# A two-layer encoder on one core: norms, weight splits, residual means and the last transposes in another order

## The chip, the cores and the metric

One core of a Trainium2 chip runs the whole kernel in one launch. The metric is the device time of that launch in microseconds. One core has TensorE (PE in the rows, with its weight loads as PEld), VectorE (DVE), ScalarE (ACT), GpSimd (POOL) and SyncE (SP); the last three can issue DMA transfers, each on a queue of its own. L611 means line 611 of the kernel before, unless the text says that it is a line of the changed one.

## The reference, cut to what matters

```python
def layer_norm(x, gain, bias):
    mean = jnp.mean(x, -1, keepdims=True)
    var = jnp.mean(jnp.square(x - mean), -1, keepdims=True)
    return (x - mean) * lax.rsqrt(var + LN_EPS) * gain + bias

def swiglu_ffn(h, w_gate, w_up, w_down):
    return (jax.nn.silu(h @ w_gate) * (h @ w_up)) @ w_down

# s5_mixer: y = C state + D u; g = gelu(y); (g * sigmoid(g @ w_glu)) @ w_out
h = concat(meta, x)                      # 16 + 1024 rows of 1024 values
for i in range(2):
    mix = s5_mixer(h, ...) if i == 0 else gqa_mixer(h, ...)
    h = layer_norm(ALPHA * h + mix, gain[i, 0], bias[i, 0])
    h = layer_norm(ALPHA * h + swiglu_ffn(h, ...), gain[i, 1], bias[i, 1])
return h[:, 16:]
```

D_FF is 2816. The inputs and all weights are float32.

## The kernel before, in words

The activations live in SBUF transposed, `acc` with 8 slices `k` of 128 features by 1040 tokens. All products run over three token tiles of 348, 348 and 344 columns (`TOK`, tiles 0, 1, 2). For accuracy every operand is a pair of a high part (rounded to fp32r) and a low part (the rest), and each of the 8 k-steps of a product takes three matmuls: high by high (L694), high by low (L695), low by high (L696). A bank of PSUM (`bk`) collects a product. `Hh` and `Hl` are the two parts of the activations.

In order of time: an S5 phase (to about 292 us) that ends with the C times state matmuls (L533, added by DVE in L535); the GLU product; the S5 output product with norm `ln0` (to about 500); FFN 0 with norm `ln1` (to about 1260); the products for K, V and Q; attention; its output product with norm `ln2` (to about 2050); FFN 1 with norm `ln3`; and the transposes and stores of the output (from about 2808).

**Order.** Nothing is scheduled by a planner: each engine executes its instructions in the order in which the program issues them. Work beside the products is written as generators. `Net.group_done` is called after each half product (four k-steps) and counts every generator down by 1.75, by 0.9 in the FFN's down products and the V rows; a generator whose count is used up runs to its next `yield`, whose value is the next count. `flush` runs a generator to its end at once. A larger number in a `yield` thus places what follows it behind more matmuls on PE's queue.

**Weights** (`class Weights`). SP loads 128 x 1024 pieces (`raw`, L592); `split` makes a unit: the high part by an ACT cast (L609) and the low part by a subtraction (L611) on DVE, or on POOL for four units of the K and V weights (`on_pool`). The w_down units are centred: ACT sums a row (L606) and writes the high part (L616), DVE the low part (L617). `tick`, called at each whole product, splits the next unit when its buffer is free.

**Norm** (`layer_norm`, one generator for each token tile). Per slice, ACT squares (L721) and POOL adds into `lns` (L723, even and odd slices apart). After a `yield` PE sums over the partitions by a matrix of ones (L735 for `s`, L736 for `q2`), ACT loads the table of ln and exp (L737) and with DVE makes 1/sqrt (L706 to L710); then for each slice DVE scales (L750), ACT writes `Hh` (L751), DVE `Hl` (L745). The mean needs no pass ahead of it since the weights and residuals are centred. For the residual the mean is taken out of `acc` later (`residual`): POOL adds the eight slices to `lnz` (L764), PE sums by ones (L768), DVE subtracts (eight L771), and in `ln1` POOL issues a save of the tile to DRAM (L774). In the last norm ACT writes into `acc` in L751 and the transposes read it.

**GLU.** The y of the S5 phase goes to DRAM (`ydram`, L543) and comes back in another layout (L554) for gelu. The last pair of feature tiles comes back late, when the GLU product already runs on the first ones (Hh by ACT in L784, Hl by DVE in L788). `centre_x` subtracts the mean from x beside it (POOL sums `sx` in L1361, PE sums by ones in L1368).

**Tail.** For each token tile the norm is flushed, then each block of 128 tokens takes two banks of four transposes (L1534); DVE copies one to `ot` (L1538), ACT the other (L1536), and SP stores the block (L1539). There are three `ot` buffers.

Of the kernel before, what the change touches and what calls it, by code (L numbers as in the profile page):

```python
# [9 lines left out]
FP32 = mybir.dt.float32  # L10
# [102 lines left out]
def s5_phase(nc, tc, P, a, ident, acc, xres, ydram, late):  # L113
# [413 lines left out]
    for ft in range(KT):  # L527
        for g0 in range(8 * ft, 8 * ft + 8, 2):
            b = bank()
            for j in range(2):  # L530
                g = g0 + j
                for c2 in range(2):
                    PE.matmul(b[:, j * NK:(j + 1) * NK], E(c2, g).rearrange("p s c -> p (s c)"), XS[:, :, c2, g],  # L533
                              start=(c2 == 0), stop=(c2 == 1))
            V.tensor_tensor(out=U[:, g0:g0 + 2, :], in0=U[:, g0:g0 + 2, :],  # L535
                            in1=b[:, :2 * NK].rearrange("p (g k) -> p g k", g=2), op=ALU.add)
        for _ in range({1: 2, 7: 1}.get(ft, 0)):
            split()
        if ft % 2:
            dst = ydram[(ft - 1) * 128:(ft + 1) * 128].rearrange("(g c) t k -> t c g k", c=CH)  # L540
            for t in range(T):
                eng = nc.gpsimd if t % 4 == 3 else nc.sync
                eng.dma_start(out=dst[t], in_=U[16 * t:16 * t + 16, 8 * ft - 8:8 * ft + 8, :])  # L543
            if ft < LATE_FT:
                for f in (ft - 1, ft):
                    ys[f] = load_y(nc.scalar, y_p, ydram, f)
                for f in (ft - 1, ft):
                    gelu(nc, acc, ys[f], f)
# [17 lines left out]
class Weights:  # L566


    def __init__(self, nc, n_units, n_raw):
        self.nc, self.nu, self.nr = nc, n_units, n_raw  # L570
        self.src = []
        self.centre = {}
        self.on_pool = set()
        self.raw = []
        self.unit = []
        self.free = []
        self.base = 0
        self.limit = 10 ** 6
# [7 lines left out]
    def dma(self):  # L586
        while len(self.raw) < min(len(self.src), len(self.unit) + self.nr):
# [7 lines left out]
            self.raw.append(r)  # L595

    def split(self):
        n = len(self.unit)
        self.dma()
# [8 lines left out]
        if c is False:  # L608
            A.copy(out=u[:, 0], in_=r)  # L609
            E = self.nc.gpsimd if n in self.on_pool else V  # L610
            E.tensor_tensor(out=u[:, 1], in0=r, in1=u[:, 0].bitcast(FP32), op=ALU.subtract)  # L611
        else:
# [6 lines left out]
        self.unit.append(u)  # L619
        self.dma()  # L620

    def tick(self):
        n = len(self.unit)
        if n < min(len(self.src), self.limit) and (n < self.nu or self.free[n - self.nu]):
            self.split()

    def get(self, n):
        while len(self.unit) <= n:
            assert len(self.unit) < self.nu or self.free[len(self.unit) - self.nu], (len(self.unit), n)
            self.split()  # L630
        return self.unit[n]

# [20 lines left out]
class Net:  # L653
    def __init__(self, nc, tc, P, a):
        self.nc, self.tc, self.P, self.a = nc, tc, P, a
        self.bg = []
        self.ln_s = {}


    def group_done(self, work=HALF, tick=True):  # L660

        if tick:
            self.w.tick()
# [11 lines left out]
    def start(self, gen, key):  # L675
        it = [gen, 0, key]
        self.bg.append(it)
        self.bg_step(it)
        return it

    def flush(self, key):
# [43 lines left out]
    def layer_norm(self, tok, ln, last=False, save=None):  # L725
# [6 lines left out]
        s, q2 = self.ln_s[tok, 0], self.ln_s[tok, 1]  # L732
        yield (3,3,3)[tok] if ln == 1 else 3.0
        v = self.bank()[:, :n]
        PE.matmul(v, self.ones, s, start=True, stop=False)  # L735
        PE.matmul(v, self.ones, q2, start=False, stop=True)  # L736
        A.preload_act_table_set("natural_log_exp_and_others")  # L737
        u = self.rstd(v, self.eps_ln, n, tp)

        def bias(k):  # L740
# [17 lines left out]

        def residual():

            yield (20.,20.,20.)[tok] if ln == 1 else 28.0
            sz = tp.tile([128, 348], FP32, tag="s", name="lnz", bufs=2)[:, :n]
            for k in range(1, KT):
                PO.tensor_tensor(out=sz, in0=x[0] if k == 1 else sz, in1=x[k], op=ALU.add)  # L764
                yield 0.9
            yield 4.0
            mz = self.bank()[:, :n]
            PE.matmul(mz, self.ones, sz, start=True, stop=True)  # L768
            for k in range(KT):
                b = self.bias_c[:, 8 * ln + k:8 * ln + k + 1]  # L770
                V.scalar_tensor_tensor(out=x[k], in0=x[k], scalar=b, in1=mz, op0=ALU.add, op1=ALU.subtract)  # L771
                yield 0.9
            if save is not None:
                nc.gpsimd.dma_start(out=save.rearrange("(k p) t -> p k t", p=128)[:, :, t0:t0 + n],  # L774
                                    in_=acc[:, :, t0:t0 + n])

        if not last:
            self.start(residual(), ("lnb", tok))

# [61 lines left out]
    def ffn(self, i, units, ln, last=False, save=None):  # L841
# [22 lines left out]
        def down(c, gt, t):  # L864
            ud = units[c][2]
            t0, n = TOK[t]
            if c == 0:
                self.flush(("lnb", t))
            for o in range(KT):
# [361 lines left out]
def whole(nc, tc, a, out):  # L1231
# [37 lines left out]
    uv = N.add_square(wq, 1280)  # L1269
    w.on_pool.update((uk + uv)[:4])  # L1270
    uq = [N.add_square(wq, 256 * i) for i in range(2)]
# [188 lines left out]
    def q_evac(o, t, b):  # L1460
        N.flush(("lnb", t))
        t0, n = TOK[t]
# [61 lines left out]
    for t in range(3):  # L1524
        N.flush(("ln", t))
        t0, n = TOK[t]
        c0 = max(t0, 16)
        while c0 < t0 + n:
            m = min(128, t0 + n - c0)
            ot = outp.tile([128, D], FP32, tag="ot", name="ot")  # L1530
# [58 lines left out]
```

## Time and profile before

| what | value |
|---|---|
| median of 3 runs | 2845.06 us (2843.23 to 2846.6) |
| profiled execution, own time | 2844.93 us |
| its span, first to last instruction | 2843.2 us |
| PE busy | 2649.4 us, 93% |
| DVE, ACT, POOL busy | 55%, 41%, 18% |
| mean granted clock of PE | 0.967 of full speed |

The profile gives one profiled execution. An engine is busy while it executes; its idle time ahead of an instruction is put down to what released it. A row with "[4.25 <-ACT Hh L784]" says that the engine sat idle 4.25 us before it, until ACT's write of Hh in L784 was done. PEclk is the clock that PE was granted, 1.00 at 2.4 GHz and 0.50 at 1.2 GHz.

### The profile page before, as it was taken

The page shows a single profiled execution, that of the slowest core. Times are in us where ns is not written, and L with a number is a line of the kernel's source. Part 1 is how long each engine was busy: PE and PEld are TensorE (multiplying, and loading weights), DVE is VectorE, ACT ScalarE, POOL GpSimd, SP SyncE. Part 2 cuts the span into 40 slices and gives each one's busy share as a digit, 9 for nine tenths or more (in the row PEclk, how much of TensorE's full clock was granted, in tenths as well). Part 3 has the DMA queues.
Part 4 walks back from the last instruction along what each step waited for, and adds up shares of the span by engine and source line. Part 5 has one row for each costly group of instructions (what it writes and reads, how often), then busy time and mean ns, then how long its engine had stood idle before and what let it go on. Part 6 is the DMA issues. An engine that isn't in the chain of part 4 may idle for free.

```text
span 2843.2 us, 43155 instructions
## 1 busy us (share of the span) xinstructions
PE 2649.4 (93%) x17277; PEld 2546.5 (90%) x17277; DVE 1559.1 (55%) x3025; ACT 1154.3 (41%) x2138; POOL 515.3 (18%) x533
## 2 busy tenths in 40 slices
PE   7657899999999999989999998999999999999997
PEld 6446899999999999988988887888999999999996
DVE  9994545733333333358768888885563333333334
ACT  7463534322212212245557778774522222222225
POOL 0770332300000000043034434431310000000002
PEclk9778999999999999999999999999999999999998
DMA  6113652221111111112111111102111111111101
GB/s 150 24 38 102 230 175 72 77 80 45 47 51 45 45 52 45 45 45 87 48 24 39 27 24 49 28 19 98 45 38 46 52 45 45 45 45 45 45 31 60
DMA packets 124836, 167.41 MB, mean 59 GB/s; under 512 B 13499, under 2 KB 104971, under 8 KB 124635
## 3 DMA queue, kind: packets, MB, share of 16 engines
q1 hardware_dynamic: 118203, 141.22, 17.5%
q0 software_dynamic: 5712, 21.30, 2.2%
q8 instruction: 136, 2.23, 0.3%
q10 hardware_dynamic: 720, 2.13, 0.2%
q14 instruction: 65, 0.53, 0.1%
HBM read 126.41 MB, written 21.23 MB: 52 GB/s over the span
## 4 chain that ended last, share of the span: by engine, by line
PE 78%; DVE 13%; ACT 4%; issue 3%; DMA 2%; POOL 1%; SPq 0%; ACTq 0%; DVEq 0%; POOLq 0%
PE bk L694 22%; PE bk L695 22%; PE bk L696 22%; PE pv L1106 4%; PE pt L1084 3%; DVE mx L1064 3%; DVE pl L1097 2%; PE b L533 2%; ACT ph L1092 1%; DVE TA L507 1%; DVE SB L508 1%; DVE XS L510 1%; PE bx L347 1%; PE b L124 1%; DVE TS L509 1%
## 5 line engine op out<-in xcount | busy, mean ns | idle before, releaser
L694 PE MATMUL bk<-Hh,unit 128*128 128x348 f32 (+1 forms) x2928 | 956.4, 327 | 9.4 <-ACT Hh L784 5.8
L695 PE MATMUL bk<-Hl,unit 128*128 128x348 f32 (+1 forms) x2928 | 945.3, 323 | 1.1 <-DVE Hl L788 1.0
L696 PE MATMUL bk<-Hh,unit 128*128 128x348 f32 (+1 forms) x2928 | 943.8, 322 | 0.0
L694 PEld LDWEIGHTS bk<-Hh,unit 128*128 128x128 f32 x2928 | 555.2, 190 | 14.7 <-ACT Hh L784 5.4
L695 PEld LDWEIGHTS bk<-Hl,unit 128*128 128x128 f32 x2928 | 554.9, 190 | 6.4 <-DVE Hl L788 2.0
L696 PEld LDWEIGHTS bk<-Hh,unit 128*128 128x128 f32 x2928 | 554.7, 189 | 0.0
L858 DVE TENSOR_TENSOR sg<-sg,bk 128x348 f32<-128x348 f32 x132 | 68.1, 516 | 632.3 <-PE bk L696 624.5
L723 POOL TENSOR_TENSOR lns<-lns,lnsq 128x348 f32<-128x348 f32 (+1 forms) x72 | 70.0, 983 | 1550.5 <-ACT lnsq L721 1549.4
L694 PE MATMUL bk<-gt,unit 128*128 128x348 f32 (+1 forms) x1056 | 340.5, 322 | 0.0
L696 PE MATMUL bk<-gt,unit 128*128 128x348 f32 (+1 forms) x1056 | 339.1, 321 | 0.0
L695 PE MATMUL bk<-gt,unit 128*128 128x348 f32 (+1 forms) x1056 | 338.5, 321 | 0.0
L881 DVE TENSOR_TENSOR acc<-acc,bk 128x348 f32<-128x348 f32 (+1 forms) x480 | 237.5, 513 | 112.7 <-PE bk L696 112.7
L860 ACT CAST gt<-sg 128x348 fp32r<-128x348 f32 x132 | 63.7, 482 | 487.6 <-DVE sg L858 487.6
L1084 PE MATMUL pt<-ident,P 128*116 128x128 f32 (+1 forms) x1188 | 181.3, 279 | 44.1 <-DVE pl L1097 39.4
L1097 DVE TENSOR_TENSOR pl<-pt,ph 116x512 fp32r<-116x512 f32 (+3 forms) x340 | 204.4, 619 | 15.0 <-ACT ph L1092 13.4
L1084 PEld LDWEIGHTS pt<-ident,P 128*116 128x116 f32 (+1 forms) x1188 | 132.5, 136 | 80.4 <-issue 30.6
L1072 POOL TENSOR_SCALAR P<-P,l 128x1044 f32<-128x1044 f32 x132 | 149.8, 1146 | 291.0 <-PE pv L1106 174.4
L694 PEld LDWEIGHTS bk<-gt,unit 128*128 128x128 f32 x1056 | 199.0, 188 | 0.5 <-issue 0.2
L695 PEld LDWEIGHTS bk<-gt,unit 128*128 128x128 f32 x1056 | 198.9, 188 | 0.5 <-issue 0.2
L696 PEld LDWEIGHTS bk<-gt,unit 128*128 128x128 f32 x1056 | 198.7, 188 | 0.0
L1092 ACT CAST ph<-pt 116x512 fp32r<-116x512 f32 (+3 forms) x340 | 168.6, 535 | 73.9 <-PE pt L1084 59.7
L609 ACT CAST unit<-raw 128x1024 fp32r<-128x1024 f32 x110 | 113.2, 1046 | 209.7 <-DMA raw<-in_ffn_w_up_dram 173.1
(287 smaller groups left out, 3928.1 us busy)
## 6 DMA issues: line engine op xcount, KB each, us to landing
raw<-in_ffn_w_gate_dram SPq DMA_DIRECT2D x44, 512.0 KB
raw<-in_ffn_w_up_dram SPq DMA_DIRECT2D x44, 512.0 KB
raw<-in_ffn_w_down_dram SPq DMA_DIRECT2D x44, 512.0 KB
y<-xdram SPq DMA_DIRECT2D x16, 520.0 KB
QA<-QH SPq DMA_DIRECT2D x30, 260.0 KB
raw<-in_attn_w_qkv_dram SPq DMA_DIRECT2D x14, 512.0 KB
xdram<-acc SPq DMA_DIRECT2D x32, 130.0 KB
xres<-xn POOLq DMA_DIRECT2D x8, 520.0 KB, 5.1
```

The source lines that it names most:

```text
L609: A.copy(out=u[:, 0], in_=r)
L694: mm(out, wh, xh, start=(first and i == 0), stop=False)
L695: mm(out, wh, xl, start=False, stop=False)
L696: mm(out, wl, xh, start=False, stop=(last and i == n - 1))
L723: (nc.vector if on_dve else nc.gpsimd).tensor_tensor(out=part, in0=part, in1=sq, op=ALU.add)
L881: V.tensor_tensor(out=x, in0=x, in1=b, op=ALU.add)
L1064: V.tensor_reduce(out=k.mx, in_=k.S[:, :, :348], axis=mybir.AxisListType.XY, op=ALU.max, negate=True)
L1072: PO.tensor_scalar(out=k.P, in0=k.P, scalar1=k.l, scalar2=1.0, op0=ALU.mult, op1=ALU.mult)
L1084: PE.transpose(b[:m, w * i + 128 * x:w * i + 128 * x + 128], u.P[x][:, KB_N * kt:KB_N * kt + m], self.ident)
L1092: A.copy(out=u.ph[s][:m, :w], in_=u.t[s][:m, :w])
L1097: V.tensor_tensor(out=u.pl[s][:m, :w], in0=u.t[s][:m, :w], in1=u.ph[s][:m, :w].bitcast(FP32), op=ALU.subtract)
L1106: PE.matmul(u.o[:, :u.w], VAs[u.j][:m, kt], (u.ph, u.pl)[x][s][:m, c:c + u.w], start=(kt == 0 and x == 0), stop=(kt == KBS - 1 and x == 1))
```

## The change

Six edits, all in the order of the work; no matmul is added or removed.

1. The eight stores of the last pair of y tiles (`ft` = 7) go round SP, POOL and ACT (3, 3 and 2 of them); before, SP issued six and POOL two. The two on ACT stand ahead of its first `Hh` casts.
2. `split` issues the cast at once, but the subtraction for the low part and the next load of raw weights only in `finish`, which the next `group_done`, `split` or `get` of the unit calls. The subtractions on POOL (`on_pool`) are gone: all are on DVE.
3. The first wait of a norm stays 3.0 for tiles 0 and 1, and becomes 7.0 (ln0, ln2) or 5.0 (ln1, ln3) for tile 2. On PE, L735 and L736 of tile 2 stand 16 k-steps behind the end of its product instead of 8 in ln0 and ln2, and 12 instead of 8 in ln1. Meanwhile `hold` keeps units of w_down from being split.
4. The three residual generators become one chain, started at the end of tile 2's norm, in the order of tiles 2, 0, 1, with shorter waits. On PE at the start of an FFN, L768 of tile 2 stands 40 k-steps behind tile 2's L736, that of tile 0 28 k-steps later and that of tile 1 24 further; in the K, V, Q stage L768 of tile 2 stands behind 16 k-steps of tile 1, tile 0's inside tile 2's K products and tile 1's inside the Q products.
5. `flush_res(t)` runs the chain until tile t is done, in place of a flush of that tile's own generator.
6. In the tail `begin` starts the waiting norm of tile 2 after the first block of tile 1.

```diff
-                eng = nc.gpsimd if t % 4 == 3 else nc.sync
+                eng = (nc.sync, nc.gpsimd, nc.scalar)[t % 3] if ft == KT - 1 else nc.gpsimd if t % 4 == 3 else nc.sync
...
+    def finish(self):
+        while self.later:
+            self.later.pop(0)()
+
     def split(self):
+        self.finish()
...
             A.copy(out=u[:, 0], in_=r)
-            E = self.nc.gpsimd if n in self.on_pool else V
-            E.tensor_tensor(out=u[:, 1], in0=r, in1=u[:, 0].bitcast(FP32), op=ALU.subtract)
+            self.later.append(lambda: V.tensor_tensor(out=u[:, 1], in0=r, in1=u[:, 0].bitcast(FP32), op=ALU.subtract))
...
-        self.dma()
+        self.later.append(self.dma)
...
     def tick(self):
         n = len(self.unit)
+        if self.hold and n in self.centre and self.centre[n] is None:
+            return
...
     def group_done(self, work=HALF, tick=True):
 
+        self.w.finish()
...
+    def begin(self, key):
+
+        for it in list(self.bg):
+            if it[2] == key and it[1] > 0 and it not in self.begun:
+                self.begun.append(it)
+                self.bg_step(it)
...
-        yield (3,3,3)[tok] if ln == 1 else 3.0
+        self.w.hold = tok == 2
+        yield 3.0 if tok < 2 else 5.0 if ln % 2 else 7.0
...
-            yield (20.,20.,20.)[tok] if ln == 1 else 28.0
...
-                yield 0.9
-            yield 4.0
+                yield 0.5
+            yield 3.0
...
-                yield 0.9
+                yield 0.6
...
-        if not last:
-            self.start(residual(), ("lnb", tok))
+            self.res_done.add(t)
+
+        def residuals():
+
+            yield 2.0
+            for t in (2, 0, 1):
+                yield from residual(t)
+
+        if not last and tok == 2:
+            self.res_done = set()
+            self.start(residuals(), "lnb")
+
+    def flush_res(self, t):
+
+        for it in list(self.bg):
+            while it[2] == "lnb" and it in self.bg and t not in self.res_done:
+                self.bg_step(it)
...
             if c == 0:
-                self.flush(("lnb", t))
+                self.flush_res(t)
...
-    w.on_pool.update((uk + uv)[:4])
...
     def q_evac(o, t, b):
-        N.flush(("lnb", t))
+        N.flush_res(t)
...
         while c0 < t0 + n:
+            if t == 1 and c0 > t0:
+                N.begin(("ln", 2))
```

How instructions stand on an engine, at three places. Lines of the changed kernel are its own: there L612 is L606 of before, L615 is L609, L621 is L616, L724 to L726 are L706 to L708, L739 is L721, L741 is L723, L756 is L737, L771 (on ACT) is L751, L785 is L764, L795 is L774, L892 and L895 (Silu and its cast) are L857 and L860, L1572 is L1536.

ACT at the start of an FFN (here ln0; ln2 reads the same), from the last square of tile 2 on; before:

```order
L721 ACTIVATE lnsq<-acc 128x344
L606 ACTIVATE unit,mean<-raw 128x1024
L616 ACTIVATE unit<-raw,mean 128x1024
L606 ACTIVATE unit,mean<-raw 128x1024
L616 ACTIVATE unit<-raw,mean 128x1024
L737 ACT_TABLE_LOAD
L706 ACTIVATE rs_y<-bk,eps_ln 128x344
L707 ACTIVATE rs_y<-rs_y 128x344
L708 ACTIVATE rs_u<-rs_y 128x344
L751 ACTIVATE Hh<-acc,small 128x344 x4
```

and changed:

```order
L739 ACTIVATE lnsq<-acc 128x344
L612 ACTIVATE unit,mean<-raw 128x1024
L621 ACTIVATE unit<-raw,mean 128x1024
L892 ACT_TABLE_LOAD
L892 ACTIVATE sg<-bk 128x348
L895 CAST gt<-sg 128x348
L756 ACT_TABLE_LOAD
L724 ACTIVATE rs_y<-bk,eps_ln 128x344
L725 ACTIVATE rs_y<-rs_y 128x344
L726 ACTIVATE rs_u<-rs_y 128x344
L771 ACTIVATE Hh<-acc,small 128x344 x2
L612 ACTIVATE unit,mean<-raw 128x1024
```

One pair of weight copies moved behind the first two writes of Hh, and a first Silu group of FFN tile 0 with a table load of its own stands ahead of the norm's table load.

POOL from the sums of tile 1 in ln1 to the residual adds of the K, V, Q stage; before:

```order
L723 TENSOR_TENSOR lns<-lns,lnsq 128x348 x3
L611 TENSOR_TENSOR unit<-raw,unit 128x1024
L723 TENSOR_TENSOR lns<-lns,lnsq 128x344 x3
L611 TENSOR_TENSOR unit<-raw,unit 128x1024
L723 TENSOR_TENSOR lns<-lns,lnsq 128x344 x3
L1450 DMA cos<-in_rope_cos_dram 128x1040
L1451 DMA sin<-in_rope_sin_dram 128x1040
L764 TENSOR_TENSOR lnz<-acc 128x348
L764 TENSOR_TENSOR lnz<-lnz,acc 128x348 x6
L774 DMA hres<-acc 128x8x348
```

and changed:

```order
L741 TENSOR_TENSOR lns<-lns,lnsq 128x348 x12
L741 TENSOR_TENSOR lns<-lns,lnsq 128x344 x6
L1484 DMA cos<-in_rope_cos_dram 128x1040
L1485 DMA sin<-in_rope_sin_dram 128x1040
L785 TENSOR_TENSOR lnz<-acc 128x344
L785 TENSOR_TENSOR lnz<-lnz,acc 128x344 x6
L795 DMA hres<-acc 128x8x344
L785 TENSOR_TENSOR lnz<-acc 128x348
L785 TENSOR_TENSOR lnz<-lnz,acc 128x348 x6
L795 DMA hres<-acc 128x8x348
```

The subtractions left POOL, and each save of a tile now stands ahead of the adds of the next one; before, the adds of the tiles 1 and 2 stood together ahead of their saves.

ACT in the tail, from the last writes of tile 1 on; before:

```order
L751 ACTIVATE acc<-acc,small 128x348 x2
L1536 COPY ot<-bk 128x512 x2
L1536 COPY ot<-bk 92x512
L737 ACT_TABLE_LOAD
L706 ACTIVATE rs_y<-bk,eps_ln 128x344
L707 ACTIVATE rs_y<-rs_y 128x344
L708 ACTIVATE rs_u<-rs_y 128x344
L751 ACTIVATE acc<-acc,small 128x344 x8
```

and changed:

```order
L771 ACTIVATE acc<-acc,small 128x348 x2
L1572 COPY ot<-bk 128x512
L756 ACT_TABLE_LOAD
L724 ACTIVATE rs_y<-bk,eps_ln 128x344
L725 ACTIVATE rs_y<-rs_y 128x344
L726 ACTIVATE rs_u<-rs_y 128x344
L771 ACTIVATE acc<-acc,small 128x344 x2
L1572 COPY ot<-bk 128x512
L1572 COPY ot<-bk 92x512
L771 ACTIVATE acc<-acc,small 128x344 x6
```

The copies of blocks 2 and 3 of tile 1 moved from ahead of tile 2's norm into the middle of its writes.

## Rows read from the trace of the kernel before

**Rows 1.** The page, busy time of each engine, share of the span, instructions.

```profile
PE 2649.4 (93%) x17277; PEld 2546.5 (90%) x17277; DVE 1559.1 (55%) x3025; ACT 1154.3 (41%) x2138; POOL 515.3 (18%) x533
```

**Rows 2.** Waits of PE; waited for: us in total, times, longest.

```profile
PE bk L1534 <- ACT acc L751: 11.4, 4, 7.9
PE bk L735 <- POOL lns L723: 11.3, 4, 4.7
PE bk L736 <- POOL lns L723: 6.7, 2, 3.3
PE bk L694 <- ACT Hh L784: 5.8, 3, 4.2
...
PE bk L694 <- ACT vf L1476: 3.6, 1, 3.6
```

**Rows 3.** Stretches of PE: from:to, us, busy (instructions), granted clock, DMA share, GB/s.

```profile
315.90:322.70 6.80, 4.17 (x13) 0.50 0.41 143
500.20:507.00 6.80, 5.23 (x16) 0.50 0.33 100
1258.00:1261.40 3.40, 3.40 (x10) 0.50 0.22 77
1271.60:1278.40 6.80, 6.00 (x17) 0.50 0.46 163
1295.50:1298.90 3.40, 3.16 (x11) 0.50 0.00 0
2049.90:2056.70 6.80, 5.67 (x18) 0.50 0.34 101
530.00:1225.00 695.00, 695.00 (x4387) 1.00 0.16 51
```

**Rows 4.** Timeline, GLU: start, us, engine, line, shapes, count, [idle before, releaser].

```profile
294.09 5.46 SPq L543 DMA_DIRECT2D ydram<-acc  x6
...
307.33 1.05 POOL L554 DMA_DIRECT2D y<-ydram  x2 [11.17 <-DMA ydram<-acc]
...
318.45 0.66 PE L694 MATMUL bk<-Hh,unit 128*128 128x348 f32 x1 [4.25 <-ACT Hh L784]
...
351.07 2.02 PE L1368 MATMUL bk<-sx,ones 128*128 128x348 f32 x6 [1.41 <-POOL sx L1361]
```

**Rows 5.** All engines, 299 to 307.3: busy (instructions), clock, DMA share, GB/s.

```profile
299.00:307.30 8.30, 8.30 (x54) 8.21 (x53) 2.89 (x6) 6.41 (x7) 0.00 (x0) 1.00 1.07 323
```

**Rows 6.** Timeline, start of FFN 0 (ln0): weights, sums, POOL's adds, scaling.

```profile
497.45 1.22 DVE L611 TENSOR_TENSOR unit<-raw,unit 128x1024 fp32r<-128x1024 f32 x1 [1.55 <-ACT unit L609]
497.58 0.84 PE L735 MATMUL bk<-lns,ones 128*128 128x344 f32 x2 [1.21 <-POOL lns L723]
501.67 0.93 POOL L764 TENSOR_TENSOR lnz<-acc 128x348 f32<-128x348 f32 x1
501.77 1.51 PE L736 MATMUL bk<-lns,ones 128*128 128x344 f32 x2 [3.34 <-POOL lns L723]
502.68 7.87 POOL L764 TENSOR_TENSOR lnz<-lnz,acc 128x348 f32<-128x348 f32 x6
...
509.79 3.47 DVE L750 SCALAR_TENSOR_TENSOR acc<-acc,small,rs_u 128x344 f32<-128x344 f32 x3
...
522.50 0.58 DVE L750 SCALAR_TENSOR_TENSOR acc<-acc,small,rs_u 128x344 f32<-128x344 f32 x1
```

**Rows 7.** Timeline, POOL around ln1: a subtraction, and six adds of tile 0.

```profile
1248.35 2.42 POOL L611 TENSOR_TENSOR unit<-raw,unit 128x1024 fp32r<-128x1024 f32 x1 [20.92 <-ACT unit L609]
...
1275.90 7.52 POOL L764 TENSOR_TENSOR lnz<-lnz,acc 128x348 f32<-128x348 f32 x6
```

**Rows 8.** The tail: a store in the chain of waits, two rows of ACT's timeline.

```profile
2816.75 7.97 DMA out_dram<-ot
...
2818.78 0.59 ACT L1536 COPY ot<-bk 128x512 f32<-128x512 f32 x1 [0.71 <-PE bk L1534]
...
2825.43 1.28 ACT L737 ACT_TABLE_LOAD   x1
```

## What was predicted

> **What bounds the kernel now.** I read the busy times first [rows 1]. TensorE (PE) works 2649.4 of 2843.2 us, 93%, and the next engine 55%. The edits remove no matmul, so they can only shorten what PE waits. Then the waits of PE [rows 2]: the five that the change touches, on the last transposes (L1534), on the sums of the norms (L735, L736), on the casts of the GLU (L694 behind Hh) and on the V rows (vf), add up to 38.8 us. Then the clock [rows 3]. Behind six of these waits the granted clock is 0.50 (1.2 GHz) for a stretch of 3.4 or 6.8 us, against 1.00 (2.4 GHz) in the run of 695 us in which PE is always busy. At half clock half of the busy time is lost: 4.17/2 = 2.1 at the GLU, 5.23/2 = 2.6 and 5.67/2 = 2.8 at the two norms ahead of an FFN, 1.7, 3.0 and 1.6 around the norm ahead of K, V and Q; 13.8 in all, 2.3 in the mean. So at most 38.8 + 13.8 = 52.6 us are to be had. A matmul of the long run takes 695.0/4387 = 0.158 us, a k-step (three of them) 0.475 [rows 3]; by this I place what is moved on PE. A half product is four k-steps, 1.9 us.
>
> The profiled execution took 2844.93 us, 0.13 under the median of 2845.06; savings read from it are taken off the median as they stand.
>
> **GLU start (A): y stores on three queues.** The six stores on SP take 5.46 us to issue, 0.91 each; POOL waits 11.17 us for all eight to land before it loads y back at 307.33, and on that load hang gelu, the Hh casts and PE's wait of 4.25 at 318.45 [rows 4]. With three left on SP they are out 3 x 0.91 = 2.7 us sooner. The two on ACT stand ahead of the first Hh casts and wait for the last addition of y on DVE (L535). An ACT issue of such a store is in no row; it may cost nothing beside that wait, or as much as SP's whole 5.46; I take SP's 0.91 for each, 1.8, so PE's first product starts that much later. If the wait of 4.25 and its slow stretch vanish, 4.25 + 2.1 − 1.8 = 4.5 is won; but the next wait, 1.41 at L1368 for POOL's sx, hangs on the same loads [rows 4] and moves by no more than they do, 2.7. I take **A = 2.7**, bounds 0 (issues dear) and 6.4 (issues free).
> How much sooner the stores land is the weak point: from 299 to 307.3 the DMA share is 1.07, all engines busy [rows 5]. The Trainium skill, "DMA: Bandwidth & Descriptors", section "Issuing engines are not separate DMA queues", speaks against this edit: transfers issued from SP, ACT and POOL run on the same 16 engines, and several issuers save issue time alone. By that, with the engines as full as the row shows, A is nothing and the time 2.7 us later.
>
> **FFN starts (B): ln0 and ln2.** PE's two matmuls of tile 2's norm now stand behind 16 k-steps instead of 8, 3.8 us later. Before, PE waited 1.21 us at L735 and 3.34 at L736, which starts at 501.77 when POOL's last sum is through [rows 6]. The squares and sums come sooner: DVE no longer waits 1.55 us for the cast of a weight unit ahead of its subtraction [rows 6], since that is issued half a product late. So the last sum ends near 500, PE arrives about then, and the waits go, 4.55, with the slow stretch (2.6 and 2.8): 7.2 each.
> What is late next is the mean for the residual (L768). Before, it stood far behind; now tile 2's stands 40 k-steps behind tile 2's L736, 19.0 us after some 501.6, at 520.6, in PE's own queue: all matmuls behind it wait too. It needs all eight L750 of that tile on DVE, then POOL's last add (0.93). Before, ACT's table load stood behind two pairs of weight copies; now behind one pair and a Silu group of about the same length, so only the sooner sums count, by 1.9 us: first L750 at 507.9 instead of 509.79. The last one ended at 522.50 + 0.58 = 523.1, so the eight take 13.3 us [rows 6]; now they end at 521.2, the add at 522.1, and PE waits 1.5. It is more if DVE and POOL hold each other up: six adds beside DVE took 7.87 (1.31 each against 0.93), and three L750 beside them 3.47 (1.16 each against 0.58) [rows 6]. Before, the last four L750 and their four L745 ran undisturbed; now tile 2's adds run beside them: 4 x 2 x (1.16 − 0.58) = 4.6, a wait of 6.1. I take 4 plus a slow stretch of 2.3: each start wins 7.2 − 6.3 = 0.9, **B = 2**. Bounds: no wait, 14.4; 6.1 + 2.3 each, −2.4.
> Here a page says more than the rows. The Trainium skill, "SBUF — State Buffer", section "SBUF: two separate sides", has VectorE and GpSimd take their shared port in turn, each for a whole instruction. By that six adds of 0.93 would stand between the DVE operations in full: a wait of 1.5 + 5.6 = 7.1, B = −4.4, the time 2840. The rows, with 1.31 and 1.16 side by side, show both slowed and neither fully stopped.
>
> **K, V, Q (C): ln1.** Here L735 waits 11.3 less 1.2 at each FFN start, so 8.9, at tiles 1 and 2 (the longest 4.7, so the other 4.2), and the V rows wait 3.6 [rows 2]; with slow stretches of 1.7, 3.0 and 1.6 that is 18.8. Four subtractions go from POOL, 2.42 each [rows 7], to DVE, 1.22 [rows 6]. For tile 1's sums I take it as even: 2.4 less on POOL, but two subtractions on DVE ahead of the values that are squared. For tile 2 the same delays the last sum by an estimated 0.7, while four more k-steps (1.9) stand ahead of it: +1.2. The norms of tiles 1 and 2 on DVE no longer run beside POOL's subtractions and adds, which doubled an L750 [rows 6]; so the wait on vf and its stretch may go, 5.2. Against that, L768 of tiles 0 and 1 now stands inside the products, while POOL first issues the save of the tile before, which waits for eight L771 on DVE: each waits 0 to 1.5 and may cost part of a slow stretch; I take 1.4 each. **C = 1.2 + 5.2 − 2.8, about 3.5**; bounds −2 (vf stays, both wait 1.5) and 12 (tile 1's sums come 2.4 sooner, tile 2's slow stretch goes too, no L768 waits).
>
> **Tail (D).** A store of 76 rows takes 7.97 us, so tile 1's last copies wait for an output buffer, and behind them on ACT stands tile 2's table load, at 2825.43 [rows 8]; PE waits 7.9 for what follows [rows 2]. Now L735 and L736 come after the first block of tile 1, and the chain from the table load stands on ACT ahead of the copies of blocks 2 and 3. The first block's copy ends at 2818.78 + 0.59 = 2819.4 [rows 8]; the load follows it, 6.0 sooner. Two copies on ACT now lie inside the chain, 2 x 0.59, and with a hand-over to DVE +1.7: 4.3 won. The stores of these blocks go out later, and the last block may wait for a buffer, 0 to 1.8. **D = 3.5**, bounds 1 and 6.
>
> Deferred subtractions and weight loads elsewhere I cost at nothing: in the long FFN run PE is always busy [rows 3], so a load issued half a product (1.9 us) later lies behind work; if that cover went, this run would show waits.
>
> **Sum:** 2.7 + 2 + 3.5 + 3.5 = 11.7; 2845.06 − 11.7 = **2833.4**. All lower bounds together −3.4, all upper ones 38.8.
>
> **Rivals.**
> 1. The means come in time: no wait at L768 at the FFN starts, B = 14.4. For it: POOL is 18% busy [rows 1] and has little else there. Against: the eight L750 end too late by 1.5 us already undisturbed. 2.7 + 14.4 + 3.5 + 3.5 = 24.1, about 2821.
> 2. The waits only change places: L768 takes at the FFN starts what L736 gave back (B = −2.4), vf is as late as before and C comes to 0, and full DMA engines leave the y loads where they are (A = 0). −2.4 + 3.5 = 1.1, about 2844. For it: the 1.5 and the 1.07 above.
> 3. Slower: the residual means hold PE wherever they stand. In the K, V, Q stage POOL starts tile 0's adds only after the save of tile 2, and tile 1's after that of tile 0, and seven adds beside DVE take 7.52 x 7/6 = 8.8 us [rows 7]. If PE stands at L768 when they start, each of the two waits 8.8 + 2.3 = 11.1, and the two FFN starts 8.4 each: 39.0. Without L768's costs the terms give 2.7 + 14.4 + 6.4 + 3.5 = 27.0; so 12 slower, about 2857. It decides from 27.0 + 5.7 = 32.7 us of L768 costs on. Against it: before, three such sets with their L768 lay in the same stage, and none shows among PE's waits.
>
> **How the numbers follow.** A measurement of this kernel can tell about 0.2%, 5.7 us, from no change: 2839.4 to 2850.7. Forecast 0.48 (2826.5 to 2839.4), rival 1 0.24 (2812 to 2826.5), rival 2 0.18 (2839.4 to 2850.7), rival 3 0.10 (over 2850.7). Faster 0.48 + 0.24 = 0.72, same 0.18, slower 0.10. The range 2815 to 2845 holds the forecast's 0.48, some 0.20 of rival 1 and 0.11 of rival 2: 0.79. It leaves out most terms at a bound at once, and rival 3.
>
> **What would show it.** In the profile after: no wait on POOL's sums at tile 2's L735 and L736 of the FFN starts, and clock 1.00 there; waits of some 4 us at L768 near 521 and 2070 instead, with a stretch at 0.50 behind. DVE, not POOL, as the engine of the low parts near 1250, and vf's wait gone. The late y loads by 305 instead of 307.33, PE's first GLU product some 1.8 us later. The last table load near 2819, the last wait of PE under 5. Wrong if L768 waits over 3 us in the K, V, Q stage, if the long FFN run shows waits, or if the ACT stores hold the Hh casts for over 3 us.

## The result, and the profile after

The changed kernel takes 2860.47 us (median of 4 runs, 2859.14 to 2865.91) against 2845.51 for the kernel before on the same chip: ratio 1.0053, 95% interval 1.0038 to 1.0068, so 15 us slower. 2833.4 was forecast; the result lies near rival 3 (2857).

The page after, the span and PE's busy time [as rows 1]:

```profile
span 2857.6 us, 43128 instructions
...
PE 2658.5 (93%) x17277; PEld 2552.7 (89%) x17277; DVE 1563.6 (55%) x3029; ACT 1156.7 (40%) x2140; POOL 509.4 (18%) x530
```

PE executes as many matmuls as before, and is busy 9 us longer. Most of that is half clock: the granted clock stood at 0.50 for 201 us, against 188 before, and half of the difference is 6.7. The waits of PE after (waited for: us, times, longest), in the lines of the changed kernel; L789 is L768 of before, L754 L735, L1570 L1534, L712 L694, L819 L784, L1402 L1368 [as rows 2]:

```profile
PE bk L789 <- POOL lnz L785: 19.3, 4, 5.7
...
PE bk L754 <- POOL lns L741: 8.1, 2, 5.2
PE bk L1570 <- ACT acc L771: 7.3, 7, 2.3
PE bk L712 <- ACT Hh L819: 6.6, 4, 2.2
...
PE bk L1402 <- POOL sx L1395: 4.7, 1, 4.7
```

The waits that were to go have shrunk: sums from 18.0 to 8.1, the last transposes from 11.4 to 7.3, vf (3.6) is gone. A wait that was not there, on the sums for the residual means, takes 19.3 in four places. The half clock that follows it shows in the stretches behind the four places [as rows 3], while the one behind ln0's sums is gone (first row):

```profile
500.20:507.00 6.80, 6.80 (x44) 1.00 0.40 122
531.90:538.80 6.90, 5.69 (x18) 0.51 0.00 0
1323.80:1330.70 6.90, 5.91 (x17) 0.51 0.00 0
1347.70:1351.10 3.40, 3.40 (x13) 0.50 0.00 0
2091.80:2098.70 6.90, 5.33 (x16) 0.51 0.01 2
```

Waits alone don't tell what a stage lost. All kernels here issue the same 12168 product matmuls in the same order, so I measured each stage as the time from the start of one of them to that of another, by its number. The columns are: GLU (0 to 576), ln0's sums (1160 to 1200), start of FFN 0 (1200 to 1500), ln1's sums and K, V (5760 to 6100), first Q products (6100 to 6324), attention (6839 to 6840, with nothing of the change in it), ln2's sums (7400 to 7480), start of FFN 1 (7480 to 7800), and from the last one to the end. The names e1 to e12 are the experiments of the next section.

| us in the profiled run | GLU | ln0 | FFN 0 start | ln1, K, V | Q | attention | ln2 | FFN 1 start | tail |
|---|---|---|---|---|---|---|---|---|---|
| before | 105.8 | 15.0 | 49.2 | 74.5 | 45.1 | 490.3 | 21.6 | 52.5 | 35.2 |
| after | 112.4 | 7.3 | 58.0 | 66.7 | 59.0 | 494.1 | 13.9 | 60.9 | 31.0 |
| e2, old means | 109.0 | 7.3 | 53.1 | 69.0 | 45.1 | 493.3 | 13.9 | 55.2 | 30.8 |
| e4, norm waits alone | 108.3 | 8.5 | 53.2 | 73.2 | 45.1 | 494.8 | 15.1 | 56.5 | 34.6 |
| e5, nothing put off | 103.5 | 8.6 | 57.6 | 69.7 | 58.5 | 490.5 | 15.1 | 60.6 | 31.0 |
| e6, means' place | 112.4 | 7.3 | 49.7 | 66.7 | 56.4 | 489.9 | 13.9 | 52.8 | 31.1 |
| e7, e2 and e5 | 104.7 | 8.6 | 52.1 | 75.4 | 45.1 | 493.2 | 15.1 | 56.7 | 31.0 |
| e8, tail alone | 107.3 | 14.8 | 49.2 | 74.4 | 45.1 | 491.5 | 21.2 | 52.5 | 31.0 |
| e9, three repairs | 104.6 | 7.3 | 49.7 | 69.0 | 45.1 | 495.0 | 13.9 | 52.8 | 30.9 |
| e10, ln1 later | 103.0 | 7.3 | 49.7 | 65.7 | 52.9 | 492.5 | 13.9 | 52.7 | 31.0 |
| e11, stores alone | 102.3 | 15.4 | 49.2 | 74.8 | 45.1 | 495.2 | 21.4 | 52.5 | 35.3 |
| e12, e9 with the old stores | 106.1 | 7.3 | 49.7 | 69.0 | 45.1 | 494.8 | 13.9 | 52.8 | 30.9 |

Attention, which no edit touches, scatters from 489.9 to 495.2, and the start of the first product from 292.7 to 296.6; the GLU of three kernels with the same code for it (before, e4, e8) from 105.8 to 108.3, and that of three others (changed, e2, e6) from 109.0 to 112.4. The other columns repeat within 0.5 us or so where the code is the same. So a difference of 4 us in attention says nothing, one of 8 at an FFN start a lot. e1 and e3 are not in the table: their first product starts only at 325.1 and 327.0, for a reason given below, and their GLU then takes 108.2 and 108.0.

From before to after: GLU +6.5, ln0 −7.7, FFN 0 start +8.8, ln1 with K and V −7.8, Q +13.9, attention +3.8, ln2 −7.7, FFN 1 start +8.3, tail −4.2, first product 0.5 later: 14.4, the difference of the two spans. The norms' sums won 23.2 in three stages, and 31.0 was lost in the stages right behind them.

### The profile page after: what moved, and what is told of

It reads as the page before. It is cut to its first block, busy times and chain, and to the rows that moved or that the text cites. A ratio compares the mean times of both kernels' runs of the same rounds, so it can differ in the third digit from the quotient of the medians.

```text
span 2857.6 us, 43128 instructions
## 1 busy us (share of the span) xinstructions
PE 2658.5 (93%) x17277; PEld 2552.7 (89%) x17277; DVE 1563.6 (55%) x3029; ACT 1156.7 (40%) x2140; POOL 509.4 (18%) x530
## 3 DMA queue, kind: packets, MB, share of 16 engines
q0 software_dynamic: 5760, 21.43, 2.2%
q8 instruction: 136, 2.23, 0.3%
## 4 chain that ended last, share of the span: by engine, by line
PE 76%; DVE 14%; ACT 5%; issue 3%; DMA 1%; POOL 1%; SPq 0%; ACTq 0%; DVEq 0%; POOLq 0%
PE bk L712 21%; PE bk L713 21%; PE bk L714 21%; PE pv L1141 4%; PE pt L1119 3%; DVE mx L1099 3%; DVE pl L1132 2%; PE b L533 2%; ACT ph L1127 1%; DVE TA L507 1%; DVE SB L508 1%; DVE XS L510 1%; DVE acc L770 1%; PE b L124 1%; PE bx L347 1%
## 5 line engine op out<-in xcount | busy, mean ns | idle before, releaser
L712 PE MATMUL bk<-Hh,unit 128*128 128x348 f32 (+1 forms) x2928 | 958.8, 327 | 6.6 <-ACT Hh L819 6.6
L712 PEld LDWEIGHTS bk<-Hh,unit 128*128 128x128 f32 x2928 | 556.3, 190 | 12.5 <-ACT Hh L819 5.2
L741 POOL TENSOR_TENSOR lns<-lns,lnsq 128x348 f32<-128x348 f32 (+1 forms) x72 | 73.1, 1023 | 1559.6 <-ACT lnsq L739 1558.4
L712 PE MATMUL bk<-gt,unit 128*128 128x348 f32 (+1 forms) x1056 | 339.9, 322 | 0.0
L895 ACT CAST gt<-sg 128x348 fp32r<-128x348 f32 x132 | 63.6, 482 | 493.5 <-DVE sg L893 493.5
L615 ACT CAST unit<-raw 128x1024 fp32r<-128x1024 f32 x110 | 113.1, 1045 | 241.4 <-DMA raw<-in_ffn_w_up_dram 182.0
L712 PEld LDWEIGHTS bk<-gt,unit 128*128 128x128 f32 x1056 | 198.6, 188 | 0.4
```

The costliest lines, as they stand in the source:

```text
L712: mm(out, wh, xh, start=(first and i == 0), stop=False)
L741: (nc.vector if on_dve else nc.gpsimd).tensor_tensor(out=part, in0=part, in1=sq, op=ALU.add)
```

## The experiments

| kernel | ratio to the kernel before | interval | about, us |
|---|---|---|---|
| changed | 1.0053 | 1.0038 to 1.0068 | +15 |
| e1_load_now | 1.0123 | 1.0108 to 1.0138 | +35 |
| e2_old_means | 0.9969 | 0.9958 to 0.9979 | −9 |
| e3_both | 1.0051 | 1.0036 to 1.0066 | +15 |
| e4_norm_waits | 0.9985 | 0.9975 to 0.9996 | −4 |
| e5_split_now | 1.0023 | 1.0013 to 1.0033 | +7 |
| e6_means_place | 0.9972 | 0.9961 to 0.9983 | −8 |
| e7_two_undone | 0.9966 | 0.9954 to 0.9977 | −10 |
| e8_tail_alone | 0.9984 | 0.9975 to 0.9993 | −5 |
| e9_best | 0.9910 | 0.9897 to 0.9924 | −26 |
| e10_ln1_later | 0.9926 | 0.9912 to 0.9939 | −21 |
| e11_stores_alone | 1.0000 | 0.9991 to 1.0008 | 0 |
| e12_old_stores | 0.9905 | 0.9888 to 0.9922 | −27 |

The kernel before took 2847.7 to 2849.1 us on the three chips of the experiments, so only ratios compare between rows, and between this table and the result.

**The GLU: e1 and e3.** In the changed kernel SP issues one load of w_glu at 250.26 where the kernel before issued two by 252.57; the second comes at 292.85, behind 18 stores of y. Timeline of before and after (L593 is L592 of before):

```profile
251.07 1.50 SPq L592 DMA_DIRECT2D raw<-in_s_w_glu_dram  x2
...
294.42 1.05 ACT L609 CAST unit<-raw 128x1024 fp32r<-128x1024 f32 x1
```

```profile
250.26 0.37 SPq L593 DMA_DIRECT2D raw<-in_s_w_glu_dram  x1
...
292.85 0.39 SPq L593 DMA_DIRECT2D raw<-in_s_w_glu_dram  x1
293.28 5.35 SPq L543 DMA_DIRECT2D ydram<-acc  x3
298.74 8.51 SPq L593 DMA_DIRECT2D raw<-in_s_w_glu_dram  x2
...
301.51 1.04 ACT L615 CAST unit<-raw 128x1024 fp32r<-128x1024 f32 x1 [6.48 <-DMA raw<-in_s_w_glu_dram]
...
302.99 0.46 PE L712 MATMUL bk<-Hh,unit 128*128 128x348 f32 x1 [2.23 <-ACT Hh L819]
```

ACT's cast of that unit moves from 294.42 to 301.51, the next Hh casts stand behind it, PE waits for them. I undid the put-off load alone.

```diff
-        self.later.append(self.dma)
+        self.dma()
```

> The changed kernel with one line undone: the next raw weights are loaded in split at once, and only the subtraction is put off. Theory (the load that was put off fell behind the y stores on SP, so ACT stands 6.5 us for raw weights of w_glu ahead of the Hh casts): the 6.6 us that the GLU lost come back, and up to 2.7 more by the three queues: 2851 to 2854, cast of the second GLU unit near 294 instead of 301.5. Rival (the two stores on ACT or the full DMA engines hold the GLU): within 2 us of the changed kernel, 2860.

> Both undone at once: raw loads at once, residual means as before. Theory: the gains add up, 2860.5 - 6.6 - 29.5 = 2824, faster than before by 21. Rival (they share a cause, for instance the order of SP's loads): 2831 or more.

Both expectations failed: e1 is 35 us slower than before, e3 as slow as the changed kernel. SP and PE of e1:

```profile
252.01 42.96 SPq L593 DMA_DIRECT2D raw<-in_s_w_glu_dram  x2
295.02 5.17 SPq L543 DMA_DIRECT2D ydram<-acc  x4
...
325.13 0.63 PE L712 MATMUL bk<-Hh,unit 128*128 128x348 f32 x1 [32.15 <-ACT Hh L819]
```

The second load cannot start before its buffer is free, and that buffer is read by the subtraction which is still put off. It stands on SP until 294.97, and behind it stand all the y stores that SP issues in the S5 phase. So the put-off load and the put-off subtraction belong together: whoever puts off the reader of a buffer puts off its next load, wherever the load is issued.

**e5: nothing put off.** Subtraction and load again behind the cast; all else as changed.

```diff
-            self.later.append(lambda: V.tensor_tensor(out=u[:, 1], ...))
+            V.tensor_tensor(out=u[:, 1], ...)
...
-        self.later.append(self.dma)
+        self.dma()
```

> The changed kernel with edit 2 undone as far as it puts things off: the subtraction (still on DVE) and the next raw load follow the cast at once. Theory (one raw load of w_glu is issued behind the y stores, and ACT's casts queue behind it): the GLU stage, 6.6 us longer than before in the changed kernel, comes to between 2.7 shorter and as long as before, while the four waits at L768 stay: 6 to 9 us slower than the kernel before instead of 15. Rival (the stores on ACT and POOL, not the load, hold the GLU): 13 to 17 slower.

Measured 7 us slower than before instead of 15: as the theory had it. The GLU takes 103.5 instead of 112.4. Over all traces it takes 109.0 to 112.4 where the load is put off (changed, e2, e6) and 103.0 to 104.7 where it is not but the stores are dealt as in the changed kernel (e5, e7, e9, e10): 4 to 9 us, 7 in the mean. The waits at L789 stay (6.23, 4.80, 3.21, 6.24).

**The means: e2 and e6.** Rows of after at the start of FFN 0 (L770 is L750 of before, L622 L617, L792 L771):

```profile
507.05 0.74 PE L754 MATMUL bk<-lns,ones 128*128 128x344 f32 x2
...
516.19 0.94 POOL L785 TENSOR_TENSOR lnz<-acc 128x344 f32<-128x344 f32 x1 [9.30 <-PE bk L714]
518.93 1.28 DVE L622 SCALAR_TENSOR_TENSOR unit<-raw,mean,unit 128x1024 fp32r<-128x1024 f32 x1 [2.88 <-ACT unit L621]
520.14 0.57 DVE L770 SCALAR_TENSOR_TENSOR acc<-acc,small,rs_u 128x344 f32<-128x344 f32 x1
...
520.85 1.13 POOL L785 TENSOR_TENSOR lnz<-lnz,acc 128x344 f32<-128x344 f32 x1 [3.73 <-DVE acc L770]
521.11 1.24 DVE L770 SCALAR_TENSOR_TENSOR acc<-acc,small,rs_u 128x344 f32<-128x344 f32 x1
...
531.94 1.11 POOL L785 TENSOR_TENSOR lnz<-lnz,acc 128x344 f32<-128x344 f32 x1 [0.52 <-DVE acc L770]
533.11 1.52 PE L789 MATMUL bk<-lnz,ones 128*128 128x344 f32 x2 [5.66 <-POOL lnz L785]
```

PE no longer waits for the sums (507.05 has no bracket) and is 5.66 us too early at L789. Between the second and the third scaling of tile 2 (L770) stands a unit of w_down that `hold` had kept back: DVE waits 2.88 us for ACT's copy of it, then takes 1.28 for the low part. In the K, V, Q stage POOL is held by the saves:

```profile
1311.35 3.95 DVE L792 SCALAR_TENSOR_TENSOR acc<-acc,bias_c,bk 128x344 f32<-128x344 f32 x8
...
1315.59 0.94 POOL L795 DMA_DIRECT2D hres<-acc  x1 [12.25 <-DVE acc L792]
1316.54 1.24 POOL L785 TENSOR_TENSOR lnz<-acc 128x348 f32<-128x348 f32 x1
1317.86 6.88 POOL L785 TENSOR_TENSOR lnz<-lnz,acc 128x348 f32<-128x348 f32 x6
...
1324.79 1.53 PE L789 MATMUL bk<-lnz,ones 128*128 128x348 f32 x2 [4.80 <-POOL lnz L785]
...
1336.93 0.91 POOL L795 DMA_DIRECT2D hres<-acc  x1 [12.19 <-DVE acc L792]
...
1346.55 0.85 PE L789 MATMUL bk<-lnz,ones 128*128 128x348 f32 x2 [3.21 <-POOL lnz L785]
```

The save waits 12.25 us on POOL for DVE's eight subtractions of tile 2, which stand behind two ropes on DVE; the adds of tile 0 start only then, when PE is already on the way.

> The changed kernel with the residual means as before: a generator for each tile, its waits of 28 or 20, and the saves where they were. Theory (the four waits at L768 of the changed kernel, 19.3 us, with a stretch at half clock behind each, are the loss): the two FFN starts give back 9.7 each and the K, V, Q stage about 10: 2831, all waits on lnz gone. Rival (POOL's adds then run beside the norm again and the sums' waits come back): above 2845.

e2 puts the three generators of before back. All waits on lnz are gone, Q takes 45.1 again, and it is 9 us faster than before: 24 back of the 29.5 expected. What is missing shows at the FFN starts, 53.1 and 55.2, 4 and 3 above before (below, e4).

e6 keeps the chain. At the FFN starts L768 of tile 2 stands 24 k-steps later; in the K, V, Q stage alone the adds of the next tile stand ahead of the save (which moves tile 0's L768 8 k-steps, tile 1's not at all).

```diff
-            yield 3.0
+            if save is not None and then is not None:
+                yield from adds(then)
+            yield 13.0 if t == 2 and save is None else 3.0
```

> The changed kernel with L768 of tile 2 placed 24 k-steps (11.4 us) later on PE at both FFN starts, and, in the K, V, Q stage alone, with POOL's adds of the next tile ahead of the save of the tile before. Theory (PE meets L768 too early at the FFN starts, and POOL stands in the save's wait for DVE with the next adds behind it): the waits of 5.66 and 5.64 and those of 4.80 and 3.21 go, with their half clock 10 at each FFN start and 10 in K, V, Q: 12 to 16 us faster than the kernel before, where the changed one is 15 slower. Rival (the adds are slow since DVE and POOL hold each other up, wherever they stand): waits of over 3 us at two or more of the four places.

8 us faster than before; 12 to 16 were expected. All four waits on lnz are gone, so it was the place of L768, not the speed of the adds: the FFN starts take 49.7 and 52.8, as before, with the 7.7 of the sums kept. What failed is Q: 56.4, since now PE waits there for the rope:

```profile
1342.15 1.05 PE L962 MATMUL bk<-rsq,blk 128*128 128x348 f32 x2 [2.38 <-ACT rsq L959]
...
1358.02 1.52 PE L962 MATMUL bk<-rsq,blk 128*128 128x344 f32 x2 [4.10 <-ACT rsq L959]
```

**e4: the norm waits alone**, on the kernel before.

```diff
-        yield (3,3,3)[tok] if ln == 1 else 3.0
+        self.w.hold = tok == 2
+        yield 3.0 if tok < 2 else 5.0 if ln % 2 else 7.0
```

> The kernel before with one edit alone: the waits of 7.0 and 5.0 ahead of the sums of tile 2, and hold. Theory (PE reaches the ones matmuls later than POOL's last sum, whoever subtracts): each FFN start wins about 7, ln1 1 to 3, 2828 to 2832. Rival (the sums come in time only since the subtraction is put off): waits of 1 us or more stay at L736, with the stretch at half clock, 2838 to 2842.

4 us faster: the size of the rival and the mechanism of neither. The sums' waits shrink to 0.6 at both FFN starts (stages of 8.5 and 15.1, against 15.0 and 21.6), without any put-off subtraction. But the FFN starts are 4 longer: the norm of tile 2 itself ends later, and the first products on tile 2 wait for its Hl:

```profile
532.36 0.42 PE L698 MATMUL bk<-Hl,unit 128*128 128x344 f32 x1 [1.02 <-DVE Hl L750]
...
534.00 0.42 PE L698 MATMUL bk<-Hl,unit 128*128 128x344 f32 x1 [0.91 <-DVE Hl L750]
```

e2 and e7 show the same wait (0.90 and 1.01), e6 and e9 do not: there POOL adds tile 2 first, and not tile 0 beside the norm of tile 2. The eight scalings of tile 2 (L770, in e4 L755) take 20.2 us in e2, e4 and e7, 16.8 in e6 and e9, and 13.3 in before. So by these stages the chain in the order 2, 0, 1 is worth some 3 us at each FFN start, once L768 stands late enough. The rest, down to 13.3, goes with the unit of w_down, for which 4.1 to 4.9 us pass between the second and the third scaling in all of these but before. PE bears it in e6 and e9; no run was made without it.

**e7: both undone.**

> The changed kernel with the means as before and with nothing put off in split: left are the stores on three queues, all subtractions on DVE, the norm waits and the tail. Theory: what the means alone gave back (9 us faster than before), and the 6.6 of the GLU on top: 13 to 16 us faster than before. Rival (the put-off subtractions are what lets the sums come in time): waits on lns at the FFN starts, 5 faster or less.

10 faster, less than expected. The GLU gave the 4, but ln1 with K and V takes 75.4 instead of e2's 69.0: the waits on vf (3.63) and on a rope (1.29) are there again. There the put-off subtraction is worth something; which of its two effects, on DVE's order or on SP's, I did not separate.

**The tail and the stores: e8, e11, e12.** Each alone on the kernel before; e12 is e9 with the old stores.

> The kernel before with the tail edit alone: the norm of tile 2 starts after the first block of tile 1. Theory: the time from the last product to the end is 4.2 us shorter, as in the changed kernel (35.16 us before, 30.95 there), and the whole 4 us shorter. Rival (the later stores at the end take it back without the other edits): under 2.

> The kernel before with the three store queues alone. Theory (SP's issues are what holds the late y loads): GLU stage 2 to 4 us shorter than in the kernel before (105.8 to 108.3 us in its profiles), 2 to 4 us faster. Rival (the stores on ACT and the full DMA engines take it back): within 1 us.

> The kernel of e9_best with the y stores dealt as before (six on SP, two on POOL). Theory (the three queues are worth nothing in the whole, as they were alone: what the GLU stage gains, the start of the GLU behind ACT's two issues loses): as fast as e9_best within 2 us, 23 to 27 us faster than the kernel before, its GLU stage 2 to 4 longer and its first product 1.5 us sooner. Rival (with the other waits gone the y loads are what PE waits for): 3 to 6 slower than e9_best.

The tail is worth 5 us alone (35.2 to 31.0 in its stage). The stores are worth nothing: e11 has a ratio of 1.0000, and e9 and e12 have 0.9910 and 0.9905. Alone they shorten the GLU in the profile, to 102.3, but the whole does not follow. Part of it is taken back ahead of the stage: in the traces of the table PE waits 2.00 before its first product where two stores are on ACT, 0.68 where none is. e12 reads the same way: its GLU takes 106.1 against 104.6 in e9, and its first product comes 1.2 sooner; with one profile each, both are within the scatter. Nor did the three stores left on SP go out sooner: they took 5.35 us (293.28 above), against 5.46 for six before [rows 4]. The Trainium skill, "DMA: Bandwidth & Descriptors", section "Issuing engines are not separate DMA queues", says that several issuers save issue time alone. The ratio of 1.0000 agrees with it, and here even that saving did not show on SP.

**e9 and e10: a version that beats both.** e9 is the changed kernel with three repairs: nothing put off for the GLU's eight units, the chain at the FFN starts with the late L768, the means of before in ln1.

```diff
         self.later.append(self.dma)
+        if n < 8:
+            self.finish()
...
-            yield 3.0
+            yield 13.0 if t == 2 else 3.0
...
-        if not last and tok == 2:
+        if ln == 1:
+            self.start(own(), ("lnb", tok))
+        elif not last and tok == 2:
```

> The changed kernel with three repairs: nothing is put off in split for the GLU's eight units; at the FFN starts the chain with L768 of tile 2 placed 24 k-steps later; in the K, V, Q stage the means as before. Theory (stage times of the earlier profiles add up): GLU 2 shorter than before, each FFN start 7.3 shorter, K, V, Q 5.4, tail 4.2: 26 us faster than the kernel before. Rival (what is won in one stage is given back in the next, as at the FFN starts of the norm waits alone): 10 to 15 faster.

2822.41 us, ratio 0.9910: 26 us faster than the kernel before, as the stages added up. The GLU, which differs from e6 by the two lines alone, goes from 112.4 to 104.6.

> The kernel of e9_best with tile 2's sums in ln1 12 k-steps later still (9.0 instead of 5.0). Theory (PE only has to come later than POOL's last sum): the wait of some 5.2 at tile 2's sums and its half clock go, 5 to 7 faster than e9_best. Rival (the norm's chain for tile 2, or the first rope or V rows, is then what PE waits for): no faster, with new waits of the same size in the K, V, Q stage.

The rival holds. In e10 the wait at tile 2's sums in ln1 is gone (3.94 in e9), and two waits on a rope take its place:

```profile
1270.70 0.85 PE L978 MATMUL bk<-rsq,blk 128*128 128x348 f32 x2 [3.88 <-ACT rsq L975]
...
1296.51 1.53 PE L978 MATMUL bk<-rsq,blk 128*128 128x348 f32 x2 [4.93 <-ACT rsq L975]
```

## Why the prediction was wrong, step by step

**A, the GLU (2.7 faster; measured 6.5 slower).** Two steps failed. The smaller one is the term for the stores: "With three left on SP they are out 3 x 0.91 = 2.7 us sooner". The three took 5.35 us, as long as the six before, and the edit alone is worth 0 (e11) and not 2.7; why three issues take as long as six, no run shows. The larger one is the last step of the working: "Deferred subtractions and weight loads elsewhere I cost at nothing", by the cover that the long FFN run gives. That run shows no waits after the change either. But the GLU start has no such cover: the units split in the S5 phase each put off a load, the second one past 18 y stores on SP, 42 us, and ACT's queue joins the load to PE's input. I looked for the hidden work in the stage where there is plenty, not in the stage where the queue that the load was moved past is full. e5 (103.5), and e9 against e6, show it: some 7 us, with 4 to 9 between single traces.

**B, the FFN starts (2 faster; measured 1.7 slower).** The first half was right: 7.2 each was forecast, 7.7 measured. For L768 I took 4 us of wait and 2.3 of clock, with a wait between 1.5 and 6.1; it was 5.66 and 5.64, and the stage lost 8.8 and 8.3. The mis-sized term is the time of the eight L750: 13.3 forecast, 514.99 to 531.80 = 16.8 measured (first and last L770 in the trace of after). The adds beside them are not what lengthened it. Four of the eight ran at 1.22 to 1.25 beside an add, and four ran at 1.13 to 1.25 in before, beside the adds of other tiles. The step that failed is "now behind one pair and a Silu group of about the same length, so only the sooner sums count": the second pair of weight copies went from ahead of the table load into the middle of the scalings, where I gave it no price, and 4.1 us pass there between the second and the third (518.93 above, and the same at 2079.21). Without it the wait would have been about 1.5, an estimate (5.66 − 4.1); no run takes it out. That the 4 us which I put down to the adds came near the measured wait is luck.

The lock that the Trainium skill describes in "SBUF — State Buffer", section "SBUF: two separate sides", fits better than I allowed: the add and the L770 shown above take 520.85 to 522.35, 1.50 together, and alone 0.94 and 0.57 (516.19 and 520.14), which is 1.51. My sentence that neither is fully stopped was read from means of mixed rows. By that page I had B = −4.4, and −1.7 was measured, between it and my +2; since by the estimate above 4.1 of each wait is the weight unit's, the size of B does not decide for or against the page.

**C, K, V, Q (3.5 faster; measured 6.1 slower).** The gains came, 7.8 for ln1, K and V against 6.4 forecast, but only in part by the steps of the forecast. vf's wait is gone, clock and all. Subtractions on DVE alone don't do that: it is 3.63 in e7. With the put-off alone 1.7 is left (e2), with the chain alone 1.5 (e5); it took both. The 1.2 for the sums came at tile 1 (4.72 to 2.83) and not at tile 2, where I had put it (4.14 to 5.23). The failing step is "each waits 0 to 1.5 and may cost part of a slow stretch; I take 1.4 each": the waits were 4.80 and 3.21, and Q lost 13.9. I had named the mechanism, a save on POOL that waits for DVE, but sized it by the adds alone, without asking when DVE would get to the subtractions: two ropes stand ahead of them, and POOL stood 12 us. Rival 3 used this price, 11.1 at each of two places; 13.9 in all came. I gave it a tenth, because three such sets lay in the stage before without a wait; but their distance to L768 on PE was just what the change altered.

**D, the tail (3.5 faster).** 4.2 in the profile, 5 alone on the chip. Right, and by its own steps: the table load comes 0.60 after the first block's copy (L1572 at 2837.33), and the longest wait behind the norm is 2.33 instead of 7.88:

```profile
2837.33 0.58 ACT L1572 COPY ot<-bk 128x512 f32<-128x512 f32 x1 [0.56 <-PE bk L1570]
2837.93 1.28 ACT L756 ACT_TABLE_LOAD   x1
```

**The chances.** The forecast's spread and its rivals turned on the norms; with B, C and D as they came and A as forecast, the stages would add up to 1 us slower than before (−2.7 + 1.7 + 6.1 − 4.2), rival 2. The put-off load, which no case held, made it a slow one; attention's 3.8 on top lies within its scatter. What the norms' sums and the tail were to give, 7.2 + 7.2 + 6.4 + 3.5 = 24, did arrive in the trace, with 27. It went into L768 (31 us in three stages: e6 gives back 16.4 of it at the FFN starts; in Q e2 gives back all 13.9, and e6 only 2.6) and the GLU (some 7, with e5 and e9).

## What to carry to other kernels

When a transfer or an operation is put off by one step, follow it at each place where that step is long or its queue is full, the first steps of a stage above all, and follow its buffer: its reader put off holds back the next load on any queue. When a matmul on a helper's result is moved forward in PE's queue, its distance has to cover the whole chain that feeds it, with the other engines' queues as they stand then (here a save that waits for DVE ahead of the next adds, and a weight unit among the scalings). Place the last link of a chain late and its first links early; a wait removed by moving work back is only won if the next consumer of that work has slack, and the stage behind must be looked at before the gain is counted.

## What the runs showed of the hardware

VectorE's scaling of one slice and GpSimd's add of the slice before it, started 0.26 us apart, took 1.50 us together, the sum of their times alone (0.57 and 0.94), and the other three such pairs of that norm 1.48 to 1.51: side by side they gained nothing. Behind each wait of 3.2 to 5.7 us at L789 the granted clock was 0.50 or 0.51 for 3.4 to 6.9 us, so that such a wait costs 5 to 9 us of stage time, more than it shows in the list of waits (an estimate: the wait and half of the stretch). Shorter waits went both ways in the same trace: behind the one of 2.23 us at 302.99 the clock stood at 0.50 for 3.4 us, behind one of 2.83 us at 1263.73 (tile 1's sums in ln1) it stayed at 1.00. Three stores of y took SP 5.35 to 5.92 us to issue in after, e5, e9 and e11, as long as six in before (5.46): the second of the three alone took 3.07 us in after.
